# Low parts of weight tiles kept in DRAM for the later token groups, and every second high part of h cast by ScalarE

## The chip, the core and the metric

One core of one Trainium2 chip. TensorE (PE) multiplies, with its weight loads on a queue of their own (PEld); VectorE (DVE), ScalarE (ACT) and GpSimd (POOL) work element by element; SyncE (SP) issues every DMA of this kernel, in one order. The metric is the device time of one execution in microseconds. Before the change it is 1192.86 us, the median of 3 runs (1191.8 to 1195.96).

## What is computed

One layer of a backbone over 2048 latent tokens and 128 prompt tokens, width 1024:

```python
h = rmsnorm(x, norm_g) * (1 + scale[:, None]) + shift[:, None]
p = h @ w_in
qkv, g_a, beta_logit, a_logit, uv, g_b, x_c, g_c, x_d, g_d = jnp.split(p, _split_points(), axis=-1)
y_a, S_new = deltanet_branch(qkv, g_a, beta_logit, a_logit, S0, conv_qkv, a_log, dt_bias, dn_norm_g)
y_b = sgu_branch(uv, g_b, sgu_norm_g, sgu_w, sgu_b)
y_c = pool_branch(x_c, g_c, pool_w, pool_scale)
y_d = fourier_branch(x_d, g_d, fourier_w)
out = jnp.concatenate([y_a, y_b, y_c, y_d], axis=-1) @ w_out
return x + gate[:, None] * out, S_new
```

The DeltaNet branch is a gated delta rule in chunks of 64 positions, scanned forward and backward; the others are a gated chunk MLP, average pooling, and a 2-D DFT. A final rmsnorm follows.

## The kernel before

**Two parts of each operand.** h and the weights are float32. For the matmuls each is split into a high part (a cast to TensorE's fp32r type) and a low part (the value minus the high part, cast again). `mm3` (L246) forms a product from three matmuls per block of 128 inputs: high by high, high by low, low by high. So every weight tile needs a high and a low part in SBUF; both are made on the chip each time the tile is loaded.

**Token groups.** The 17 token tiles of 128 are worked in three groups: group 0 and group 1 with 6 tiles, group 2 with 4 latent tiles and the prompt. Only one group's h lies in SBUF (`hT`, high and low).

**Stages.** Phase A runs over the groups 0, 1, 2: `x_prep` and `x_fin` make h, then come the projections for the DFT and the scalars (`wxd`, 272 columns), the pooling branch (`wxc_d`, two tiles) and q, k, v (six tiles of `in_wt`), with the short convolution (L824), the chunk matrices and the triangular solve (L725, L727) on DVE. The second stage loads the other ten tiles of `in_wt` and `wv` (256 columns) for group 2, then group 1, then group 0 (`gates`, `r_b`); beside it runs the scan (`scan`), whose 34 steps read R and C from DRAM. Last come the 17 output tiles. So each tile of `in_wt` and `wxc_d`, and `wv`, is loaded three times, once for each group.

**The load of a weight tile.** `load_w` (L218) takes one of three slots (`Ring`) in `BIG`, 136 columns each, or two for a wide tile. It brings the tile in halves of 4 input blocks to a staging tile `wst`, of which there are two buffers; casts it into the slot (ACT in phase A, L242; DVE after it, L240); and subtracts to get the low part (L243: DVE for the first half, POOL for the second). The cast waits until TensorE is done with the slot's tile of three loads ago; the next DMA into a `wst` buffer waits until the subtract has read it.

**The split of h.** For each of the 8 blocks f of 128 features, `x_fin` transposes on PE, ACT writes h (L351), and `h_split` (L358) casts the high part on DVE (L361) and subtracts on DVE for even f, on POOL for odd f (L362).

**What sets the order.** The program is written stage by stage, and a scheduler places the instructions of each engine by a timeline of its own and by priorities (`tc.high_priority`). Each engine then runs its list in order, SP's DMAs too.

## Time and profile before

| | us |
|---|---|
| median of 3 runs | 1192.86 |
| the profiled execution | 1198.78 |
| its span, first to last instruction | 1197.0 |
| PE busy in the span | 1046.3 |
| DVE busy | 818.9 |
| POOL busy | 433.2 |
| ACT busy | 386.2 |

Busy time is that of one execution. Matmuls are pipelined and their ends are modelled, so a busy PE is not one at its peak, and shares of a whole span mix stages with different limits: what a change in a stage is worth is read from the rows of that stage.

### The profile page before, as it was taken

The page shows a single profiled execution, that of the slowest core. Times are in us where ns is not written, and L with a number is a line of the kernel's source. Part 1 is how long each engine was busy: PE and PEld are TensorE (multiplying, and loading weights), DVE is VectorE, ACT ScalarE, POOL GpSimd, SP SyncE. Part 2 cuts the span into 40 slices and gives each one's busy share as a digit, 9 for nine tenths or more (in the row PEclk, how much of TensorE's full clock was granted, in tenths as well). Part 3 has the DMA queues.
Part 4 walks back from the last instruction along what each step waited for, and adds up shares of the span by engine and source line. Part 5 has one row for each costly group of instructions (what it writes and reads, how often), then busy time and mean ns, then how long its engine had stood idle before and what let it go on. Part 6 is the DMA issues. An engine that isn't in the chain of part 4 may idle for free.

```text
span 1197.0 us, 27975 instructions
## 1 busy us (share of the span) xinstructions
PE 1046.3 (87%) x11351; PEld 954.6 (80%) x11351; DVE 818.9 (68%) x1837; ACT 386.2 (32%) x734; POOL 433.2 (36%) x436
## 2 busy tenths in 40 slices
PE   4689897888768789967988999888999889999997
PEld 1489786888757788955778888878899879999997
DVE  1547878699995799958865533672443398887765
ACT  1345566436675564131131111121111311111211
POOL 1338446633562245511132132232144444332212
PEclk7599897898978899988899999999999889999998
DMA  9799557854453655565268356578555655444331
GB/s 309 238 327 290 156 117 202 250 165 112 107 134 103 154 126 126 179 170 160 71 197 241 100 170 207 176 230 283 143 151 161 204 153 186 132 142 140 108 131 71
DMA packets 251395, 204.16 MB, mean 171 GB/s; under 512 B 109150, under 2 KB 218718, under 8 KB 251010
## 3 DMA queue, kind: packets, MB, share of 16 engines
q1 hardware_dynamic: 251266, 202.37, 57.7%
q8 instruction: 89, 1.46, 0.5%
q14 instruction: 40, 0.33, 0.1%
HBM read 138.86 MB, written 63.46 MB: 169 GB/s over the span
## 4 chain that ended last, share of the span: by engine, by line
PE 41%; DVE 27%; DMA 17%; issue 6%; ACT 4%; SPq 2%; POOL 2%; DVEq 0%; ACTq 0%; POOLq 0%
PE pj L250 32%; DMA wst<-in_wt_dram 4%; PE pa L1035 3%; DMA ada<-in_ada_dram 3%; DVE LL L727 3%; DVE acc L824 3%; DVE ltmp L725 3%; DMA pr<-in_cpr_dram 2%; DVE BIG L243 2%; DVE BIG L361 1%; DVE acc L871 1%; SPq L1024 1%; DVE BIG L240 1%; DVE BIG L362 1%; DVE LL L748 1%
## 5 line engine op out<-in xcount | busy, mean ns | idle before, releaser
L250 PE MATMUL pj<-BIG 128*128 128x256 f32 (+4 forms) x3888 | 630.8, 319 | 25.6 <-ACT raw L805 5.6
L250 PEld LDWEIGHTS pj<-BIG 128*128 128x128 f32 x3888 | 578.1, 201 | 50.7 <-issue 11.0
L250 PE MATMUL pj<-BIG,yh 128*128 128x256 f32 x1088 | 196.7, 286 | 1.6 <-ACT BIG L1340 0.8
L243 POOL TENSOR_TENSOR BIG<-wst,BIG 128x512 fp32r<-128x512 f32 (+1 forms) x66 | 93.3, 1414 | 215.2 <-DVE BIG L240 131.2
L250 PEld LDWEIGHTS pj<-BIG,yh 128*128 128x128 f32 x1088 | 164.7, 191 | 4.6 <-ACT BIG L1340 1.0
L250 PE MATMUL pj<-BIG,yl 128*128 128x256 f32 x544 | 140.8, 284 | 0.0
L250 PEld LDWEIGHTS pj<-BIG,yl 128*128 128x128 f32 x544 | 99.0, 191 | 0.4
L240 DVE CAST BIG<-wst 128x512 fp32r<-128x512 f32 (+2 forms) x72 | 35.0, 487 | 75.7 <-DMA wst<-in_wt_dram 35.4
L1398 POOL TENSOR_TENSOR z<-z,xs 128x1024 f32<-128x1024 f32 x16 | 40.3, 2521 | 75.8 <-DVE z L1390 66.0
L1042 POOL TENSOR_TENSOR gS<-S,sc_s 128x256 f32<-128x256 f32 x32 | 19.7, 616 | 132.1 <-DVE S L1057 109.1
L824 DVE SCALAR_TENSOR_TENSOR acc<-raw,prm,acc 128x768 f32<-128x768 f32 (+2 forms) x72 | 66.3, 942 | 1.6 <-ACT acc L822 1.6
L243 DVE TENSOR_TENSOR BIG<-wst,BIG 128x512 fp32r<-128x512 f32 (+1 forms) x66 | 49.8, 754 | 24.3 <-ACT BIG L242 20.7
L1359 ACT ACTIVATE yh<-yt 128x768 fp32r<-128x768 f32 (+1 forms) x34 | 20.5, 628 | 121.6 <-issue 65.5
L1204 ACT ACTIVATE g<-pj 128x256 f32<-128x256 f32 (+1 forms) x64 | 23.0, 397 | 109.6 <-PE pj L250 109.3
L725 DVE TENSOR_TENSOR ltmp<-LL 128x60 f32<-128x60 f32 (+14 forms) x90 | 55.5, 617 | 1.6
L727 DVE TENSOR_TENSOR LL<-LL,ltmp 128x60 f32<-128x60 f32 (+14 forms) x90 | 55.3, 615 | 1.5
L242 ACT ACTIVATE BIG<-wst 128x512 fp32r<-128x512 f32 (+1 forms) x60 | 37.7, 633 | 38.4 <-DMA wst<-in_wt_dram 17.9
L264 PE MATMUL pb<-ada,c 128*32 128x256 f32 x192 | 22.1, 566 | 31.7 <-DMA ada<-in_ada_dram 21.4
L1057 DVE TENSOR_TENSOR S<-pa,gS 128x256 f32<-128x256 f32 x34 | 14.3, 421 | 50.6 <-PE pc L1035 45.3
L1390 DVE TENSOR_TENSOR z<-pj,gbc 128x256 f32<-128x256 f32 x68 | 26.2, 420 | 29.1 <-PE pj L250 28.8
L362 POOL TENSOR_TENSOR BIG<-h,BIG 128x384 fp32r<-128x384 f32 (+2 forms) x28 | 29.1, 1041 | 44.5 <-DVE BIG L361 38.7
L1360 DVE TENSOR_TENSOR yl<-yt,yh 128x768 fp32r<-128x768 f32 (+1 forms) x34 | 40.4, 1206 | 4.1 <-ACT yh L1359 3.9
(280 smaller groups left out, 1690.2 us busy)
## 6 DMA issues: line engine op xcount, KB each, us to landing
wst<-in_wt_dram SPq DMA_DIRECT2D x96, 256.0 KB, 3.7
R<-rec_d SPq DMA_DIRECT2D x136, 128.0 KB, 3.0
ada<-in_ada_dram SPq DMA_DIRECT2D x24, 512.0 KB, 8.7
C<-com_d SPq DMA_DIRECT2D x68, 128.0 KB, 3.2
xs<-xs_d SPq DMA_DIRECT2D x16, 512.0 KB, 5.3
out_dram<-z SPq DMA_DIRECT2D x16, 512.0 KB, 3.0
x<-in_xs_dram SPq DMA_DIRECT2D x13, 512.0 KB, 6.4
xs_d<-x SPq DMA_DIRECT2D x13, 512.0 KB, 4.7
```

The costliest lines, as they stand in the source:

```text
L240: nc.vector.tensor_copy(hi[:, ks, a:a + w], st[:, :, :w])
L242: nc.scalar.activation(hi[:, ks, a:a + w], st[:, :, :w], AF.Copy)
L243: (nc.vector if k0 == 0 else nc.gpsimd).tensor_tensor(lo[:, ks, a:a + w], st[:, :, :w], hi[:, ks, a:a + w].bitcast(F32), op=ALU.subtract)
L250: nc.tensor.matmul(out, lh[a](k), rh[b](k), start=(k == first and i == 0), stop=(k == last and i == 2))
L362: (nc.gpsimd if f % 2 else nc.vector).tensor_tensor(hT[1][:, f, off:off + w], h, hi.bitcast(F32), op=ALU.subtract)
L725: nc.vector.tensor_tensor(tv, X[:, :, j, j + 1:32].unsqueeze(2).to_broadcast([128, 2, j, ni]), bc(X[:, :, 0:j, j], ni), op=ALU.mult)
L727: nc.vector.tensor_tensor(X[:, :, 0:j, j + 1:32], X[:, :, 0:j, j + 1:32], tv, op=ALU.add)
L824: nc.vector.scalar_tensor_tensor(o, raw[:, si + j:si + j + n], w[:, j:j + 1], o, op0=ALU.mult, op1=ALU.add)
L1035: nc.tensor.matmul(ps[o, q], lh(q)[hp], rh[hp, q])
L1360: nc.vector.tensor_tensor(yl[:, q], yt[:, q], yh[:, q].bitcast(F32), op=ALU.subtract)
L1390: nc.vector.tensor_tensor(z[:, ns], ps, gbc[:, cd, ns], op=ALU.mult)
L1398: nc.gpsimd.tensor_tensor(z, z, xs, op=ALU.add)
```

## The change

**Low parts.** When a tile of `in_wt`, `wxc_d` or `wv` is loaded for the first time, its low part is made as before and then stored to a DRAM tile `lo_d` of its own. When it is loaded again, `load_w` issues a DMA of the low part from DRAM straight to the slot ahead of the two `wst` DMAs, and leaves out the subtracts. `wxd` (272 columns) stays as it was. There are 19 stores and 38 such loads: 36 of a tile of 128 columns (512 KB by the sizes of its type) and two of `wv`, of 1 MB.

**h.** In `h_split`, ACT casts the high part for even f; DVE keeps the odd ones.

```diff
+            key = str(src)
+            kept = key in lo_d
+            if kept:
+                nc.sync.dma_start(out=lo.bitcast(F32), in_=lo_d[key])
...
-                    (nc.vector if k0 == 0 else nc.gpsimd).tensor_tensor(lo[:, ks, a:a + w], st[:, :, :w], hi[:, ks, a:a + w].bitcast(F32), op=ALU.subtract)
-            return hi, lo
+                    if not kept:
+                        (nc.vector if k0 == 0 else nc.gpsimd).tensor_tensor(lo[:, ks, a:a + w], st[:, :, :w], hi[:, ks, a:a + w].bitcast(F32), op=ALU.subtract)
+        if n != 272 and not kept:
+            lo_d[key] = dram.tile([128, KC, n], F32, name=f"lo_d{len(lo_d)}")
+            nc.sync.dma_start(out=lo_d[key], in_=lo.bitcast(F32))
+        return hi, lo
...
-        nc.vector.tensor_copy(hi, h)
+        if f % 2:
+            nc.vector.tensor_copy(hi, h)
+        else:
+            nc.scalar.activation(hi, h, AF.Copy)
```

**Counts by engine.** DVE's L243 goes from 66 to 26 instructions, POOL's from 66 to 26; DVE's L361 from 56 to 28, and ACT gains the other 28. SP gains 57 DMAs. ACT's table loads go from 44 to 48, since its list has another order. Changed lines of the new kernel: L236 is the load of a low part, L251 its store, L242 the `wst` DMA, L372 and L374 the casts of h on DVE and ACT, L375 the subtract of h.

**What moves: SP in phase A, the q, k, v and pooling weights of group 1.** In a row's brackets stand the semaphores it waits for; DMAHW ones are earlier DMAs. Before:

```order
L238 DMA wst<-in_wt_dram 128x4x128 [waits DMAHW2_49,DVE_49]
L302 DMA xs_d<-x 128x1024 [waits DMAHW1_49,Pool_49]
L238 DMA wst<-in_wt_dram 128x4x128 [waits Pool_49]
L302 DMA xs_d<-x 128x1024 [waits DMAHW4_49,DMAHW3_49,Pool_49]
L887 DMA raw_d<-rawc 128x768 [waits DVE_49,Activation_49]
L238 DMA wst<-in_wt_dram 128x4x128 [waits DMAHW5_49,DMAHW0_49,Pool_49]
L238 DMA wst<-in_wt_dram 128x4x128 [waits DMAHW6_49,DMAHW2_49,DVE_49]
```

After, at the same place:

```order
L236 DMA BIG<-lo_d_1093 128x8x128 [waits DMAHW6_49,PE_49]
L242 DMA wst<-in_wt_dram 128x4x128 [waits DMAHW7_49,Activation_49]
L242 DMA wst<-in_wt_dram 128x4x128 [waits DMAHW1_49,DMAHW0_49,Activation_49]
L900 DMA raw_d<-rawc 128x768 [waits DVE_49]
L577 DMA pf_d_85<-pt 48x2x64 [waits DMAHW2_49,Activation_49]
L236 DMA BIG<-lo_d_1103 128x8x128 [waits DMAHW3_49,PE_49]
L312 DMA xs_d<-x 128x1024 [waits DMAHW4_49,Pool_49]
L242 DMA wst<-in_wt_dram 128x4x128 [waits DMAHW7_49,DMAHW5_49,Activation_49]
```

The `wst` DMAs now wait for ACT's cast instead of a subtract on DVE or POOL, and the DMA of a low part, which waits for PE to leave the slot, stands between them.

**What moves: SP in the second stage, group 1, beside the scan's R and C.** Before:

```order
L1026 DMA C<-com_d 128x256 [waits DMAHW6_49,PE_49]
L1026 DMA C<-com_d 128x256 [waits DMAHW7_49]
L238 DMA wst<-in_wt_dram 128x4x128 [waits DMAHW0_49,DVE_49]
L1024 DMA R<-rec_d_78 64x512 [waits DMAHW1_49,PE_49]
L1024 DMA R<-rec_d_78 64x512 [waits DMAHW2_49]
L1024 DMA R<-rec_d_80 64x512 [waits DMAHW3_49]
L1024 DMA R<-rec_d_80 64x512 [waits DMAHW4_49]
L238 DMA wst<-in_wt_dram 128x4x128 [waits DMAHW5_49,DMAHW0_49,DVE_49]
```

After:

```order
L1039 DMA C<-com_d 128x256 [waits PE_49]
L1039 DMA C<-com_d 128x256
L236 DMA BIG<-lo_d_6462 128x8x128 [waits DMAHW4_49,PE_49]
L242 DMA wst<-in_wt_dram 128x4x128 [waits DMAHW5_49,DVE_49]
L242 DMA wst<-in_wt_dram 128x4x128 [waits DMAHW6_49,DMAHW1_49,DVE_49]
L1037 DMA R<-rec_d_78 64x512 [waits DMAHW7_49,PE_49]
L1037 DMA R<-rec_d_78 64x512 [waits DMAHW0_49]
L1037 DMA R<-rec_d_80 64x512
L1037 DMA R<-rec_d_80 64x512 [waits DMAHW2_49]
L236 DMA BIG<-lo_d_5591 128x8x128 [waits DMAHW3_49,PE_49]
```

The low part stands ahead of the R loads of a scan step, with a wait for PE of its own.

**What moves: DVE and ACT where `x_fin` makes h of group 1.** DVE before (acc is the short convolution, kt, Pp and S belong to the scalars of group 0):

```order
L361 CAST BIG<-h 128x384 x2
L362 TENSOR_TENSOR BIG<-h,BIG 128x384
L824 SCALAR_TENSOR_TENSOR acc<-raw,prm,acc 128x768
L361 CAST BIG<-h 128x384
L824 SCALAR_TENSOR_TENSOR acc<-raw,prm,acc 128x768
L601 TENSOR_REDUCE kt<-tm 128x12
L824 SCALAR_TENSOR_TENSOR acc<-raw,prm,acc 128x768
L243 TENSOR_TENSOR BIG<-wst,BIG 128x4x136
L361 CAST BIG<-h 128x384
```

ACT after, at this place:

```order
L361 ACTIVATE h<-pa,modab 128x384
L374 ACTIVATE BIG<-h 128x384
L246 ACTIVATE BIG<-wst 128x4x136
L361 ACTIVATE h<-pc,modab 128x384
L615 ACT_TABLE_LOAD
L615 ACTIVATE kt<-kt,eps 128x12
L246 ACTIVATE BIG<-wst 128x4x136
L818 ACTIVATE raw<-pj 128x392
L374 ACTIVATE BIG<-h 128x384
```

Every second cast of h stands now in ACT's list, in between its casts of weights, its evictions of PSUM (L818) and its writes of h.

## Rows read from the trace of the kernel before

**Rows 1.** The page: the chain of work that ended last, by engine and by line, as shares of the span.

```profile
PE 41%; DVE 27%; DMA 17%; issue 6%; ACT 4%; SPq 2%; POOL 2%; DVEq 0%; ACTq 0%; POOLq 0%
...
by line: PE pj L250 32.3%; issue 5.8%; DMA wst<-in_wt_dram 4.4%; PE pa L1035 3.3%; DMA ada<-in_ada_dram 2.7%; DVE LL L727 2.6%; DVE acc L824 2.6%; DVE ltmp L725 2.5%; DMA pr<-in_cpr_dram 2.1%; DVE BIG L243 1.9%; DVE BIG L361 1.1%; DVE acc L
```

**Rows 2.** Busy time of each engine in stretches of 50 us (PE, PEld, DVE, ACT, POOL with the number of instructions, then TensorE's granted clock as a share of full speed, the DMA engines' share and GB/s). The first two lie in group 0's part of phase A, the next five in the rest of it, the last two in the second stage.

```profile
150.00:200.00 50.00, 43.16 (x308) 38.50 (x308) 41.02 (x73) 34.09 (x52) 25.40 (x27) 0.86 0.71 170
200.00:250.00 50.00, 40.84 (x376) 38.70 (x376) 36.92 (x65) 21.90 (x40) 30.29 (x29) 0.93 0.73 222
250.00:300.00 50.00, 45.81 (x335) 43.11 (x334) 49.29 (x93) 25.53 (x43) 17.87 (x16) 0.93 0.47 117
300.00:350.00 50.00, 35.52 (x258) 31.22 (x256) 49.63 (x82) 33.24 (x52) 27.09 (x29) 0.84 0.55 130
350.00:400.00 50.00, 41.76 (x630) 37.77 (x631) 30.22 (x90) 26.27 (x56) 17.11 (x24) 0.84 0.42 100
400.00:450.00 50.00, 42.93 (x466) 41.01 (x466) 47.45 (x97) 30.67 (x60) 21.90 (x27) 0.87 0.64 147
450.00:500.00 50.00, 47.19 (x328) 46.10 (x328) 48.65 (x89) 16.01 (x31) 30.08 (x44) 0.97 0.52 143
650.00:700.00 50.00, 46.06 (x619) 42.15 (x621) 27.93 (x71) 6.58 (x16) 15.97 (x14) 0.97 0.40 117
850.00:900.00 50.00, 50.00 (x735) 46.89 (x735) 21.63 (x45) 6.92 (x17) 18.18 (x16) 1.00 0.50 148
```

**Rows 3.** Groups of instructions by line and shape: count, busy time in us, mean of one in ns, then the idle time ahead of them.

```profile
L243 POOL TENSOR_TENSOR BIG<-wst,BIG 128x512 fp32r<-128x512 f32 x54 | 75.9, 1406 | 167.7 <-DVE BIG L240 86.7 <-ACT BIG L242 33.0 <-PE pj L250 21.9
L243 DVE TENSOR_TENSOR BIG<-wst,BIG 128x512 fp32r<-128x512 f32 x54 | 41.4, 766 | 20.8 <-ACT BIG L242 18.0 <-PE pj L250 1.8
L242 ACT ACTIVATE BIG<-wst 128x512 fp32r<-128x512 f32 x48 | 29.9, 627 | 33.9 <-DMA wst<-in_wt_dram 17.9 <-PE pj L250 11.6 <-DMA wst<-wxc_d 4.3
L826 ACT ACT_TABLE_LOAD x12 | 15.4, 1283 | 0.7 <-DVE acc L824 0.5
L351 ACT ACTIVATE h<-pa,modab 128x384 f32<-128x384 f32 x16 | 10.5, 666 | 1.9 <-PE pa L349 1.6 <-POOL BIG L362 0.3
```

**Rows 4.** All instructions of L243 in stretches of 50 us (DVE and POOL busy, then clock, DMA share, GB/s), the two pairs of stretches of Rows 2 in which DVE is nearly full; and their sum over the whole execution.

```profile
250.00:300.00 50.00, 2.73 (x4) 6.87 (x4) 0.93 0.47 117
300.00:350.00 50.00, 2.10 (x3) 4.02 (x3) 0.84 0.55 130
400.00:450.00 50.00, 3.13 (x4) 6.25 (x4) 0.87 0.64 147
450.00:500.00 50.00, 6.21 (x6) 7.46 (x5) 0.97 0.52 143
...
sum 1200.00, DVE 49.76 POOL 93.26; mean DVE 2.07 POOL 3.89
```

**Rows 5.** The casts of L361 on DVE in the stretches from 0 to 650 us, summed.

```profile
sum 650.00, DVE 27.01; mean DVE 2.08
```

**Rows 6.** Waits of SP's queue for others, and of PE for the low parts: us in total, times, longest.

```profile
SPq L238 <- DVE BIG L243: 89.1, 26, 10.0
SPq L238 <- POOL BIG L243: 68.5, 40, 3.9
SPq L1024 <- PE pc L1035: 28.8, 15, 5.0
...
PE pj L250 <- DVE BIG L243: 5.4, 4, 2.9
```

**Rows 7.** DMA issues: count, KB each, median us from issue to landing.

```profile
wst<-in_wt_dram SPq DMA_DIRECT2D x96, 256.0 KB, 3.7
R<-rec_d SPq DMA_DIRECT2D x136, 128.0 KB, 3.0
out_dram<-z SPq DMA_DIRECT2D x16, 512.0 KB, 3.0
x<-in_xs_dram SPq DMA_DIRECT2D x13, 512.0 KB, 6.4
xs_d<-x SPq DMA_DIRECT2D x13, 512.0 KB, 4.7
```

**Rows 8.** The chain from 371 to 376 us, where group 2's weights come in: start, duration, what.

```profile
371.21 0.64 ACT BIG L242
371.87 0.70 DVE BIG L243
372.59 3.06 DMA wst<-in_wt_dram
375.68 0.64 ACT BIG L242
```

**Rows 9.** The timeline of the second stage, group 0: start, duration, instruction. 23 matmul records are those of one chunk of 24.

```profile
871.86 0.43 DVE L240 CAST BIG<-wst 128x512 fp32r<-128x512 f32 x1 [3.57 <-PE pj L250]
...
873.80 2.99 PE L250 MATMUL pj<-BIG 128*128 128x256 f32 x23
878.05 1.28 POOL L243 TENSOR_TENSOR BIG<-wst,BIG 128x512 fp32r<-128x512 f32 x1 [2.95 <-PE pj L250]
...
879.29 3.98 POOL L1250 TENSOR_TENSOR u<-u,g 128x768 f32<-128x768 f32 x2
...
880.69 0.89 DVE L240 CAST BIG<-wst 128x512 fp32r<-128x512 f32 x1 [1.08 <-DMA wst<-in_wt_dram]
```

More of the change, by code (lines that the diff above doesn't have):

```diff
@@ L242, in load_w @@
                         nc.scalar.activation(hi[:, ks, a:a + w], st[:, :, :w], AF.Copy)
-                    (nc.vector if k0 == 0 else nc.gpsimd).tensor_tensor(lo[:, ks, a:a + w], st[:, :, :w], hi[:, ks, a:a + w].bitcast(F32), op=ALU.subtract)
-            return hi, lo
+                    if not kept:
[4 more added lines that the diff above has]
+        return hi, lo
+    lo_d = {}
     def mm3(out, lh, rh, ks=range(KC), first=0, last=KC - 1):
```

## Prediction

> **What bounds the kernel now.** I read the chain of work first, then the stretches, then the groups that the change touches. The chain [rows 1] is no single engine's: PE has 41% of it, DVE 27%, DMA 17%. The stretches say where each rules [rows 2]. From 250 to 350 us and from 400 to 500 us DVE is busy 47.45 to 49.63 of 50 us, while PE has gaps and its granted clock falls to 0.84: there DVE is the bound. From 350 to 400 us nothing is full (DVE 30.22, ACT 26.27): h and the weights of group 2 are made step after step. In the second stage PE rules: 46.06 and 50.00 of 50, with DVE at 21 to 28. The output tiles load no weight through the changed code and keep their time. So the change can pay in phase A for groups 1 and 2, where DVE is full and tiles are loaded for the second and third time; in group 0 it only adds, and in the second stage it can easily cost, since PE's list has little slack there.
>
> **Part 1: subtracts that go.** 40 leave DVE and 40 leave POOL. At 766 and 1406 ns [rows 3] that is 40 x 0.766 = 30.6 us of DVE and 40 x 1.406 = 56.2 us of POOL. By place: 16 of the 38 kept loads lie in phase A (six q, k, v tiles and two pooling tiles, for two groups), with one DVE subtract each: 16 x 0.766 = 12.3 us. The other 22 loads, with 24 DVE subtracts (`wv` has two), are in the second stage: 18.4 us.
>
> What is worth what? The whole line has 49.76 us on DVE [rows 4], and 1.9% of 1197.0 = 22.7 us of it stands on the chain [rows 1], a share of 0.46. For phase A this gives 12.3 x 0.46 = 5.6 us as a low value. In the two full stretches the line has 14.17 us, its four stretches summed [rows 4], most of it of kept tiles, and where an engine is full nearly all that leaves it is gained: 12.3 us as a high value. I take 8. In the second stage PE is next in line at once. The share of 0.46 would give 18.4 x 0.46 = 8.5 us, a full PE 0; I take 3.
>
> The staging loop belongs to this term, and is not counted again. Today a turn is cast 0.64, subtract 0.70, DMA 3.06 us [rows 8], and SP waits for subtracts for 89.1 and 68.5 us before it may refill `wst` [rows 6]. A kept tile frees the buffer at the cast, 0.7 us sooner; the low part's DMA ahead of it takes about this back.
>
> POOL's 56.2 us matter in another way: the same cast took 0.43 us alone and 0.89 us while POOL worked on L1250 [rows 9]. If part of the DVE work beside those subtracts ran slower for them, it speeds up. Low end 0; high end 56.2 x 0.46 x half a DVE's pace = 12.9; I take 2, nearer to the low end, since the two casts are a single pair.
>
> **Part 2: casts of h.** Half of 27.01 us [rows 5] leaves DVE: 13.5 us. On the chain L361 has 1.1% = 13.2 us, a share of 0.49: 6.6 us saved at most. ACT gets 28 casts at about its own price for that shape, 0.63 to 0.67 us by L242 and L351 [rows 3], some 17 us, and in `x_fin` the cast now stands on the engine that also writes the next h. For two features ACT had 2 x 0.666 and DVE two casts and a subtract; after it ACT has 2 x 0.666 + 0.63 = 1.96 us, so ACT becomes as late as DVE was. Where DVE is full this gains, where `x_fin` sets the pace (350 to 400 us) it does not: between +6 of cost (ACT's queue ahead of a cast) and -6.6; I take a gain of 2.
>
> The other order of ACT's list has four more table loads, 4 x 1.283 = 5.1 us [rows 3]. ACT is busy 16 to 34 of 50 us in phase A [rows 2], so most of this is covered; cost 1, between 0 and 5.1. The Trainium skill (ScalarE: Activation LUTs, What ACT_TABLE_LOAD costs) puts a drain of some 1.38 us to each load, so that a switch is about 2.66 us. By it the four would be an estimated 10.6 us of ACT, and I would put 2 where I put 1, so the sum would be 1 us less of a gain.
>
> **Part 3: stores of low parts.** 19 DMAs on SP, eight of them in group 0, where the DMA engines are busy 0.71 to 0.73 of the time [rows 2], each behind both subtracts of its tile, which the next `wst` DMA waits for today. Nobody waits for the data until the next group, 100 us later. What they can delay is the DMAs behind them: one of this size lands in 3.0 to 6.4 us [rows 7]. If nothing of it shows, 0; if in group 0 each holds up the next by what it lands later than a `wst`, 4.7 - 3.7 = 1.0 us, 8; I take 2.
>
> **Part 4: loads of low parts.** Each waits on SP until PE has left the slot, then has to land before the third matmul of the tile. For most tiles there is time: with three slots, in phase A at least a whole tile of two chunks (48 matmuls) lies between the release of a slot and its next use, and the slots in the second stage have at least 48 matmuls, 2 x 2.99 = 6.0 us by the time of one chunk [rows 9] and scan steps besides, except one. The second `gates` tile after `wv` takes a slot that `wv` leaves, and is needed one chunk later: 3.0 us. There the present work fits: two casts and POOL's subtract, 2 x 0.43 + 1.28 = 2.1 us. A DMA of this size takes 3.0 (output), 4.7 (`xs_d`) or 6.4 us (x, at the crowded start): PE stands still for 0, 1.7 or 3.4 us, once in group 1 and once in group 0. I take the middle one: 2 x 1.7 = 3.4. For the 8 tiles with two chunks of time, 4.7 us fits and 6.4 is late by 0.4: 0 to 3. The low part of `wv`, 1 MB, I cost at nothing: it comes at the change of groups, where `r_load` brings h back by 8 DMAs and splits it on DVE, and PE needs that too; without this cover it would be a landing, some 4.7 us, twice. [...]
>
> These 22 loads are also in front of the scan's R and C on SP and on the DMA engines. R lands in 3.0 us [rows 7], and SP already waits 28.8 us in all for PE ahead of R [rows 6]. Cost 1, with the upper end under the second rival.
>
> **The sum.** Gains 8 + 3 + 2 + 2 = 15; costs 1 + 2 + 3.4 + 1 = 7.4. That is 7.6 us less than the profiled execution's 1198.78: 1191.2. The profiled execution was 5.9 us above the median of the runs, 1192.86; taken off that, 1185.3, and I say 1185.
>
> **Rivals.** *First: nothing to be seen.* PE waits for the low parts for only 5.4 us directly [rows 6], and the order of every list changes. If phase A gives the low value, 5.6, and nothing else, against the 7.4 of cost, the time is 1192.86 + 1.8 = 1194.7; with the second stage's 3 as well, 1191.7. For it: the second stage is PE's [rows 2]. Against it: two stretches of 100 us where DVE is full.
>
> *Second: slower, by the scan's supply.* Mechanism: in the second stage the low part's DMA stands ahead of R and C in SP's list, waits for PE's last use of a slot, and then moves four times as much as one R (512 against 128 KB [rows 7]). If R lands after the scan step asks for it, PE, which runs its list in order, stops with it. Each of the 22 loads would cost up to 4.7 - 3.0 = 1.7 us, 37 us if all did; with half, 19 us, less the 7.6 + 1 of the sum's other terms: about 1203. It decides from the point where the delay of R exceeds the slack of a scan step; since steps are spaced by PE's own work there, I take it for less likely. For it: SP is one queue, and PE is full.
>
> *Third: the full gain.* If DVE is as much the bound as the four stretches say, 12.3 in phase A, 6.6 from h and 8.5 in the second stage, and the low parts land in 3.0 us: 27.4 - 4 = 23.4 less, 1169.5.
>
> *That it does not do what it says* can be excluded for the counts: the lists of the new kernel have the 38 loads and 26 subtracts.
>
> **Chances.** My forecast, 1176 to 1189: 0.40. Full gain, under 1176: 0.14. Nothing to be seen, within 0.3% (about 3.6 us, what a measurement of this kernel can tell from no change): 0.19. Slower: 0.27, of which most ends below 1206. So faster 0.54, same 0.19, slower 0.27. The range for 8 in 10 runs from 1167 to 1206: it leaves out a part of the slower case and a little of the full gain.
>
> **What would show it.** Right: the DVE stretches of phase A for groups 1 and 2 shorter, the first scan step some 8 us earlier in time, SP's waits for L243 cut by more than half, PE without new waits for a DMA of `lo_d` but for one or two of 1 to 3 us behind `wv`. The cast of h: ACT in 350 to 400 us fuller, without PE waiting longer for h's low parts. Wrong: PE waiting for `lo_d` in many places of the second stage, or for R and C; the granted clock lower there; or group 0 longer by more than a few us, by its stores. The sum would also fail if the new lists put other work of DVE in front of the solve, since each engine runs in order and a term here takes the rest of the order as it was.

## The result, and the profile after

The changed kernel takes 1212.85 us, the median of 20 runs (1203.0 to 1222.85), against 1195.09 for the kernel before in as many. The ratio is 1.0143, 95% interval 1.0123 to 1.0163: slower by 17 us, where 8 us of gain were forecast. The second rival's side came true. The profiled execution was one of the two slowest of the 20, 1221.22 us at a mean granted clock of 0.910, 8.4 us above the median; so its rows are read for where the time goes, not for sums, and beside those of e2 below, which has the same low parts (1210.24 us, clock 0.918).

The page of the changed kernel: busy time, DMA traffic, and the chain by engine.

```profile
PE 1049.1 (86%) x11351; PEld 961.4 (79%) x11351; DVE 765.3 (63%) x1769; ACT 402.1 (33%) x766; POOL 372.5 (31%) x396
...
DMA packets 310675, 235.62 MB, mean 193 GB/s; under 512 B 110062, under 2 KB 277998, under 8 KB 310290
...
PE 47%; DVE 20%; DMA 17%; ACT 7%; issue 4%; SPq 3%; POOL 1%; DVEq 0%; ACTq 0%; POOLq 0%
```

DVE lost 53.6 us of work and POOL 60.7; by the counts it was 30.6 + 13.5 = 44.1 and 56.2, so what stayed on DVE ran 9.5 us quicker too. In the chain DVE fell from 27% [rows 1] to 20%, and PE rose from 41% to 47%.

The same stretches as in [rows 2], of the changed kernel.

```profile
150.00:200.00 50.00, 38.77 (x267) 33.53 (x265) 38.68 (x68) 33.56 (x56) 24.20 (x26) 0.78 0.85 212
200.00:250.00 50.00, 45.89 (x399) 44.46 (x400) 30.94 (x62) 25.11 (x46) 26.03 (x25) 0.88 0.85 252
250.00:300.00 50.00, 47.38 (x369) 45.54 (x368) 46.16 (x88) 29.09 (x46) 17.88 (x18) 0.97 0.69 172
300.00:350.00 50.00, 34.28 (x236) 31.54 (x236) 42.44 (x79) 38.64 (x65) 18.91 (x26) 0.80 0.56 128
350.00:400.00 50.00, 41.29 (x733) 37.29 (x731) 21.09 (x75) 25.82 (x59) 10.35 (x17) 0.90 0.63 153
400.00:450.00 50.00, 45.95 (x425) 43.46 (x414) 48.48 (x111) 32.68 (x65) 17.07 (x28) 0.97 0.84 200
450.00:500.00 50.00, 47.03 (x325) 46.15 (x324) 49.20 (x80) 14.02 (x23) 30.51 (x44) 0.97 0.72 209
650.00:700.00 50.00, 50.00 (x647) 45.40 (x641) 20.95 (x79) 8.79 (x24) 2.46 (x4) 1.00 0.59 173
850.00:900.00 50.00, 45.13 (x563) 41.94 (x561) 15.60 (x35) 6.58 (x15) 8.30 (x9) 0.92 0.71 193
```

Read DVE's number, the third with a count behind it, and the clock, the third number from the end. From 300 to 400 us DVE is busy 42.44 and 21.09 of 50 where it was 49.63 and 30.22. In 650 to 700 us PE is full. In 850 to 900 us, where PE was busy 50.00 at a clock of 1.00, it is now busy 45.13 at 0.92, with the DMA engines at 0.71 instead of 0.50.

Groups of the changed lines: count, busy us, mean ns, then the idle time ahead of them.

```profile
L248 POOL TENSOR_TENSOR BIG<-wst,BIG 128x512 fp32r<-128x512 f32 (+2 forms) x26 | 38.1, 1466 | 92.8 <-DVE BIG L244 48.6 <-issue 31.5 <-ACT BIG L246 6.3
L248 DVE TENSOR_TENSOR BIG<-wst,BIG 128x512 fp32r<-128x512 f32 (+2 forms) x26 | 20.9, 804 | 8.7 <-ACT BIG L246 8.4
L374 ACT ACTIVATE BIG<-h 128x384 fp32r<-128x384 f32 (+2 forms) x28 | 13.0, 464 | 0.2
L372 DVE CAST BIG<-h 128x384 fp32r<-128x384 f32 (+2 forms) x28 | 12.0, 430 | 27.7 <-ACT h L361 27.7
```

DMA issues: count, KB, median us from issue to landing (compare [rows 7]).

```profile
wst<-in_wt_dram SPq DMA_DIRECT2D x96, 256.0 KB, 4.6
BIG<-lo_d SPq DMA_DIRECT2D x36, 512.0 KB, 5.5
R<-rec_d SPq DMA_DIRECT2D x136, 128.0 KB, 3.4
lo_d<-BIG SPq DMA_DIRECT2D x18, 512.0 KB, 5.9
```

The trace tells the landing of 13 of the 38 loads of low parts: 5.5 us after the issue in the median, 4.1 to 8.9 in all. `wst` went from 3.7 to 4.6, R from 3.0 to 3.4. Waits, as in [rows 6]:

```profile
SPq L1037 <- PE pc L1048: 51.4, 15, 7.7
SPq L242 <- DVE BIG L248: 27.5, 12, 8.5
SPq L242 <- POOL BIG L248: 13.0, 10, 2.7
...
PE pc L359 <- ACT h L361: 15.4, 4, 6.0
PE pj L260 <- DMA BIG<-lo_d: 10.5, 4, 4.1
```

SP's waits for subtracts fell from 89.1 and 68.5 us to 27.5 and 13.0. Three waits are new or longer: PE stands 10.5 us before low parts and 15.4 before an h that ACT has not written, and SP waits 51.4 us instead of 28.8 for PE ahead of R. With the low parts alone (e2) PE stands 9.8 us before low parts and 11.7 before h, where before the change it is 4.3 before h, and SP waits only 31.5 us ahead of R.

Group 0's part of the second stage, the chain by line. Before, from 797 to 951 us:

```profile
by line: PE pj L250 59.0%; PE pa L1035 11.7%; DMA wos<-in_wo_dram 6.3%; DMA wst<-in_wt_dram 5.0%; DMA R<-rec_d 3.3%; issue 2.6%; DVE r L1047 2.0%; PE pc L1035 1.9%; PE pb L1258 1.9%; ACT BIG L1340 1.4%; DVE BIG L1198 1.0%; DVE BIG L1341 0.8
```

After, from 801 to 975 us, with some of its pieces (start, us, what):

```profile
by line: PE pj L260 43.6%; DMA BIG<-lo_d 11.1%; PE pa L1048 7.9%; DMA wst<-in_wt_dram 6.8%; DMA R<-rec_d 4.8%; DMA wos<-in_wo_dram 3.6%; DMA raw_d<-yd 2.7%; issue 2.6%; PE pb L1271 2.2%; DVE r L1060 1.9%; SPq L1037 1.9%; DVE BIG L244 1.3%; 
...
801.81 7.65 DMA BIG<-lo_d
864.85 6.79 DMA BIG<-lo_d
923.20 4.94 DMA BIG<-lo_d
```

The load of a low part is now on the path, with 11.1% of 174 us, some 19 us. These are the places where PE stands for one there (start, us, instruction, and in brackets how long PE stood):

```profile
809.51 2.70 PE L260 MATMUL pj<-BIG 128*128 128x256 f32 x12 [4.10 <-DMA BIG<-lo_d]
871.69 1.65 PE L260 MATMUL pj<-BIG 128*128 128x256 f32 x6 [2.31 <-DMA BIG<-lo_d]
928.18 1.09 PE L260 MATMUL pj<-BIG 128*128 128x256 f32 x7 [3.88 <-DMA BIG<-lo_d]
```

The first load, issued at 801.81, is the low part of `wv`, 1 MB. The last, issued at 923.20, came 1.1 us before PE asked for it (928.18 - 3.88 = 924.30). It had not waited for its slot: in the 6 us before, SP had waited 2.9 us for a `wst` DMA to land and 1.8 us for DVE's cast, for a `wst` DMA ahead of it in its list.

To compare kernels part by part, I count the projections' matmuls (`pj` from `BIG`, 3888 in all) in order of time: the first 1560 are phase A's, then 600, 864 and 864 of the second stage's groups 2, 1 and 0. Each number below is the time from the start of one part's first matmul to the next part's, in us, phase A's from the start of the span; the rest is the end of the scan and the output tiles, up to the start of the last matmul on a `pj` tile.

| kernel | phase A | group 2 | group 1 | group 0 | rest |
|---|---|---|---|---|---|
| before | 463.5 | 156.3 | 176.9 | 153.9 | 237.8 |
| after | 455.6 | 168.3 | 177.8 | 173.4 | 235.7 |
| e1_h_only | 465.4 | 143.0 | 183.6 | 159.0 | 241.5 |
| e2_low_only | 446.9 | 155.1 | 187.6 | 175.9 | 234.3 |
| e3_low_phase_a | 447.4 | 147.3 | 185.0 | 152.7 | 241.5 |
| e4_low_second | 462.2 | 150.4 | 170.6 | 164.3 | 243.3 |
| e5_stores_only | 456.8 | 157.9 | 174.8 | 157.0 | 238.4 |
| e6_second_firsts | 464.4 | 151.7 | 171.4 | 160.2 | 239.8 |
| e7_second_seconds | 460.3 | 158.2 | 177.1 | 161.3 | 241.3 |
| e8_h_all | 454.9 | 153.1 | 178.4 | 152.2 | 241.8 |
| e9_second_half | 460.9 | 149.6 | 173.6 | 156.0 | 241.3 |
| e10_second_pool_queue | 462.9 | 147.3 | 180.7 | 165.3 | 239.4 |
| e11_phase_a_and_h | 455.9 | 150.9 | 184.4 | 152.2 | 240.3 |
| e12_phase_a_h_all | 454.6 | 146.6 | 186.4 | 151.4 | 240.5 |
| e13_phase_a_second_half | 449.7 | 155.9 | 187.8 | 153.9 | 240.2 |
| e14_h_phase_a | 464.6 | 144.5 | 186.8 | 157.8 | 241.4 |
| e15_h_second | 463.2 | 158.9 | 176.8 | 156.8 | 237.6 |
| e16_h_odd | 460.6 | 151.7 | 185.4 | 153.5 | 241.9 |
| e17_phase_a_second_stores | 445.3 | 157.4 | 184.5 | 147.1 | 237.4 |
| e18_second_half_stores | 445.0 | 150.6 | 174.4 | 157.6 | 237.3 |

In the changed kernel phase A is 7.9 us shorter; group 2's part of the second stage is 12.0 us longer and group 0's 19.5. Two of these kernels are others once more (e14 is e1, e15 is the kernel before, see below), and by them a part repeats to within some 3 us. A part also holds whatever else the lists put between its bounds. Group 0's part before and after, with the columns of [rows 2]:

```profile
796.70:950.60 153.90, 141.66 (x1913) 132.28 (x1908) 63.50 (x136) 28.59 (x70) 56.05 (x46) 0.97 0.62 191
```

```profile
801.70:975.10 173.40, 151.54 (x2007) 140.20 (x2005) 60.80 (x131) 30.35 (x75) 42.70 (x38) 0.95 0.71 210
```

Of the 19.5 us, 9.9 are PE busy, with 94 matmuls more in this part and a clock of 0.95 instead of 0.97; the other 9.6 are PE idle, and the three waits above (10.3 us) are as much.

### The profile page after: what moved, and what is told of

It is laid out like the page before. It is cut to its first block, busy times and chain, and to the rows that moved or that the text cites. A ratio compares the mean times of both kernels' runs of the same rounds, so it can differ in the third digit from the quotient of the medians.

```text
span 1219.4 us, 27942 instructions
## 1 busy us (share of the span) xinstructions
PE 1049.1 (86%) x11351; PEld 961.4 (79%) x11351; DVE 765.3 (63%) x1769; ACT 402.1 (33%) x766; POOL 372.5 (31%) x396
## 2 busy tenths in 40 slices
DMA packets 310675, 235.62 MB, mean 193 GB/s; under 512 B 110062, under 2 KB 277998, under 8 KB 310290
## 4 chain that ended last, share of the span: by engine, by line
PE 47%; DVE 20%; DMA 17%; ACT 7%; issue 4%; SPq 3%; POOL 1%; DVEq 0%; ACTq 0%; POOLq 0%
PE pj L260 37%; PE pa L1048 3%; DMA wst<-in_wt_dram 3%; DVE ltmp L738 3%; DVE LL L740 2%; DMA pr<-in_cpr_dram 2%; DVE acc L837 2%; DMA R<-rec_d 2%; DMA ada<-in_ada_dram 2%; DMA BIG<-lo_d 2%; ACT XF L770 1%; SPq L1037 1%; PE pb L1271 1%; DMA h_d<-h 1%; DVE LL L731 1%
## 5 line engine op out<-in xcount | busy, mean ns | idle before, releaser
L260 PE MATMUL pj<-BIG 128*128 128x256 f32 (+4 forms) x3888 | 631.3, 319 | 45.3 <-DMA BIG<-lo_d 10.5
L260 PEld LDWEIGHTS pj<-BIG 128*128 128x128 f32 x3888 | 579.9, 201 | 68.5 <-issue 14.3
L244 DVE CAST BIG<-wst 128x512 fp32r<-128x512 f32 (+2 forms) x72 | 40.5, 566 | 77.6 <-DMA wst<-in_wt_dram 36.6
L837 DVE SCALAR_TENSOR_TENSOR acc<-raw,prm,acc 128x768 f32<-128x768 f32 (+2 forms) x72 | 62.7, 893 | 7.4 <-ACT acc L835 7.3
L248 POOL TENSOR_TENSOR BIG<-wst,BIG 128x512 fp32r<-128x512 f32 (+2 forms) x26 | 38.1, 1466 | 92.8 <-DVE BIG L244 48.6
L738 DVE TENSOR_TENSOR ltmp<-LL 128x60 f32<-128x60 f32 (+14 forms) x90 | 58.7, 652 | 1.6
L1066 ACT ACTIVATE xn<-pa 128x256 f32<-128x256 f32 x34 | 13.0, 383 | 123.7 <-PE pa L1048 123.3
L740 DVE TENSOR_TENSOR LL<-LL,ltmp 128x60 f32<-128x60 f32 (+14 forms) x90 | 50.9, 566 | 1.7
L1373 DVE TENSOR_TENSOR yl<-yt,yh 128x768 fp32r<-128x768 f32 (+1 forms) x34 | 43.8, 1310 | 5.0 <-ACT yh L1372 5.0
L375 POOL TENSOR_TENSOR BIG<-h,BIG 128x384 fp32r<-128x384 f32 (+2 forms) x28 | 28.3, 1012 | 53.3 <-DVE BIG L372 47.5
```

The lines of the kernel that those rows point to most:

```text
L244: nc.vector.tensor_copy(hi[:, ks, a:a + w], st[:, :, :w])
L248: (nc.vector if k0 == 0 else nc.gpsimd).tensor_tensor(lo[:, ks, a:a + w], st[:, :, :w], hi[:, ks, a:a + w].bitcast(F32), op=ALU.subtract)
L260: nc.tensor.matmul(out, lh[a](k), rh[b](k), start=(k == first and i == 0), stop=(k == last and i == 2))
L375: (nc.gpsimd if f % 2 else nc.vector).tensor_tensor(hT[1][:, f, off:off + w], h, hi.bitcast(F32), op=ALU.subtract)
L738: nc.vector.tensor_tensor(tv, X[:, :, j, j + 1:32].unsqueeze(2).to_broadcast([128, 2, j, ni]), bc(X[:, :, 0:j, j], ni), op=ALU.mult)
L740: nc.vector.tensor_tensor(X[:, :, 0:j, j + 1:32], X[:, :, 0:j, j + 1:32], tv, op=ALU.add)
```

## The experiments

Each kernel was timed beside the kernel before on the same chip; a ratio is to that kernel, with its 95% interval.

### The two halves of the change

Each is one part of the diff alone on the kernel before: the cast of h (**e1_h_only**), and the low parts (**e2_low_only**), these again only where a tile's first load is in phase A, or only after it:

```diff
-        if n != 272 and not kept:
+        if n != 272 and not kept and not Ring.late:   # e3_low_phase_a
+        if n != 272 and not kept and Ring.late:       # e4_low_second
```

> Only the cast of h: every second high part of h on ScalarE, no low part kept. Theory A (the loss is the supply of low parts in the second stage): about as before, 1193 to 1197 us, ratio 0.998 to 1.002. Theory B (ScalarE's cast delays h at the start of groups 1 and 2, as the trace of the changed kernel suggests with PE waiting 11.9 us for h between 190 and 340 us): 5 to 12 us slower, ratio 1.004 to 1.010. Theory C (the stores and their traffic): as A.

> Only the low parts kept in DRAM, all casts of h on VectorE as before. Theory A and C: most of the loss is here, ratio 1.012 to 1.020. Theory B: half of it or less, ratio under 1.008.

> Low parts kept for the tiles of phase A alone (8 stores, 16 loads), subtracts in the second stage as before, casts of h as before. Theory A: faster than before by the 8 us that phase A gained in the trace, ratio 0.990 to 0.996. Theory C (stores and traffic cost as much as the subtracts): ratio 0.999 to 1.005.

> Low parts kept for the tiles of the second stage alone (11 stores, 22 loads), phase A as before, casts of h as before. Theory A: the whole loss and more, ratio 1.014 to 1.022, with PE waiting some 10 us for the loads of low parts and the span of group 0's part of the second stage up by about 20 us. Theory B or C: under 1.008.

| kernel | median us | ratio |
|---|---|---|
| e1_h_only | 1203.80 | 1.0070 (1.0044 to 1.0096) |
| e2_low_only | 1204.13 | 1.0071 (1.0043 to 1.0100) |
| e3_low_phase_a | 1182.54 | 0.9891 (0.9853 to 0.9928) |
| e4_low_second | 1205.66 | 1.0086 (1.0054 to 1.0118) |

Both halves lose, and together make the whole loss (1.0070 x 1.0071 = 1.0141, measured 1.0143). The low parts are two changes in one: in phase A they gain 1.1%, in the second stage they lose 0.9%. Their product, 0.9976, is not what both give together, 1.0071. Waits of PE for low parts in e4:

```profile
PE pj L260 <- DMA BIG<-lo_d: 8.6, 4, 3.4
```

### Stores without loads

**e5_stores_only**: the 19 stores are issued and nothing is loaded back; all subtracts stay.

> All 19 stores of low parts, but no load of one: every subtract stays. Theory S (the stores and their traffic cost): ratio 1.003 to 1.010. Theory W or T (it is the loads in the second stage): 0.998 to 1.003, under 3 us.

1197.91 us against 1195.48, ratio 1.0036 (1.0008 to 1.0064): the stores cost 2.4 us on their own by the medians, 4.3 by the ratio, and 1 to 8 by its interval.

### Which loads of the second stage, and why

Tiles are loaded in pairs there. **e6_second_firsts** keeps the first of each pair and `wv`, **e7_second_seconds** the second, which takes the slot that was left last. **e9_second_half** keeps only blocks 4 to 7 of each low part, **e10_second_pool_queue** issues whole loads from GpSimd:

```diff
-                nc.sync.dma_start(out=lo.bitcast(F32), in_=lo_d[key])
+                nc.sync.dma_start(out=lo[:, 4:].bitcast(F32), in_=lo_d[key][:, 4:])   # e9, with `if not kept or k0 == 0:` for the subtract
+                nc.gpsimd.dma_start(out=lo.bitcast(F32), in_=lo_d[key])               # e10
```

> Second stage alone, and there only the first tile of each pair and wv kept: 6 stores, 12 loads (two of 1 MB). Their slots are free a whole pair before they are needed. Theory W (a low part lands later than PE needs it, where a slot comes free one or two chunks ahead): no loss, ratio 0.993 to 1.001, and no wait of PE for a low part. Theory T (the traffic and the place in SP's list, whatever the tile): more than half of the 1.0086 of all 22 loads, 1.004 to 1.008.

> Second stage alone, and there only the second tile of each pair kept: 5 stores, 10 loads, those whose slot comes free one or two chunks ahead of their use. Theory W: all of the loss, ratio 1.007 to 1.014, with PE waiting 8 to 12 us for low parts. Theory T: less than half of it, 1.001 to 1.005.

> Second stage only, and of each low part only blocks 4 to 7 are kept and loaded (256 KB instead of 512 KB); blocks 0 to 3 are subtracted on DVE as in the kernel before. If the loss of the second stage (ratio 1.0086 with whole low parts) comes from PE standing before a low part that has not landed, most of it goes: the bytes are halved and their first use comes 12 matmuls (some 1.5 us by 2.99 us for a chunk of 24) later, so PE waits under 2 us for `lo_d` in all, and the ratio is 0.999 to 1.004. If it comes from the DMA's place in SP's list ahead of R, C and `wst`, the place stays and the ratio stays at 1.005 to 1.009, with few waits for `lo_d`.

> Low parts kept in the second stage only, as in the run that gave 1.0086, but their 22 loads are issued by GpSimd and not by SyncE: SP's list has no wait for a slot ahead of R, C and `wst`. By the queue theory the loss goes: ratio under 1.003, SP's wait for PE ahead of R back near 28.8 us or below. By the landing theory it stays: the load can still not start before PE has left the slot, so PE waits 8 us or more for `lo_d` and the ratio is 1.006 or more. GpSimd may add its own: its list waits for PE, and the scan's work behind it is late.

| kernel | median us | ratio |
|---|---|---|
| e6_second_firsts | 1200.58 | 1.0045 (1.0018 to 1.0072) |
| e7_second_seconds | 1207.38 | 1.0090 (1.0058 to 1.0122) |
| e9_second_half | 1192.50 | 0.9992 (0.9961 to 1.0023) |
| e10_second_pool_queue | 1206.25 | 1.0093 (1.0058 to 1.0129) |

Waits of PE for low parts, first of e6, then of e7:

```profile
PE pj L261 <- DMA BIG<-lo_d: 1.7, 1, 1.7
```

```profile
PE pj L261 <- DMA BIG<-lo_d: 14.5, 3, 7.2
```

Landing of the loads in e4 and in e9, us from issue, smallest, median and largest (the traces tell it for 8 of 22 loads in e4 and for 2 of 22 in e9):

```profile
DMA to landing us min/median/max: 3.9/5.5/6.9
```

```profile
DMA to landing us min/median/max: 3.5/3.6/3.6
```

And in e10 the waits, and the landing of a load:

```profile
POOL BIG L236 <- PE pj L260: 69.9, 12, 11.8
PE pj L260 <- DMA BIG<-lo_d: 7.4, 7, 1.5
...
BIG<-lo_d POOLq DMA_DIRECT2D x20, 512.0 KB, 7.0
```

The seconds of the pairs lose most, with PE standing 14.5 us in three places; 10 loads of them cost as much as all 22. Halves are asked for half a chunk later, and the two that can be read landed in 3.6 us: no wait of PE for `lo_d` is left in e9, and the loss is gone, though e9 halves the bytes of the loads too. GpSimd's queue frees SP's list of the loads and doesn't help, but it is no clean test of SP's list: GpSimd itself waits 69.9 us for PE, a load then takes 7.0 us, and PE still stands 7.4 us. So most of the loss of the second stage goes with PE standing before a low part that has not landed. That a load could not start earlier is not shown. In e7, where PE stands longest, SP comes to the load only behind four R of a scan step, does not wait for PE there, and PE asks for the low part 0.1 us after the issue. PE, then SP:

```profile
834.26 1.65 PE L261 MATMUL pj<-BIG 128*128 128x256 f32 x6 [7.16 <-DMA BIG<-lo_d]
```

```profile
823.64 3.28 SPq L1035 DMA_DIRECT2D R<-rec_d  x4
827.02 0.55 SPq L236 DMA_DIRECT2D BIG<-lo_d  x1
```

So the place in SP's list is a part of the cause: not R late behind the loads, but a load late behind R. And waits of PE are not the whole loss: e6 loses 0.45% with only 1.7 us of them, which its expectation had given to the traffic and the place in SP's list.

### Casts of h

On the kernel before: all high parts on ACT (**e8_h_all**), every second one in phase A only (**e14_h_phase_a**) or in the second stage only (**e15_h_second**), and the odd features on ACT (**e16_h_odd**). The edits of e14 and e15 do not part anything: all 56 casts of `h_split` lie in phase A (L361, 48.5 to 374.5 us of the kernel before), and in the second stage `r_load` splits h by lines of its own. So e14 is the program of e1, and e15 that of the kernel before, with the same lists. On the kernel with low parts kept in phase A: the cast of the change (**e11_phase_a_and_h**), and all casts (**e12_phase_a_h_all**).

```diff
+        if f % 2:                       # e1, e11: even f on ACT
+        if f % 2 or Ring.late:          # e14
+        if f % 2 or not Ring.late:      # e15
+        if f % 2 == 0:                  # e16
             nc.vector.tensor_copy(hi, h)
+        else:
+            nc.scalar.activation(hi, h, AF.Copy)   # e8, e12: always
```

> No low part kept; ScalarE casts all the high parts of h, not every second one (double dose). If ScalarE's queue is what the cast of h costs: twice the loss, ratio 1.012 to 1.020. If the loss of the half dose came from the new order of the lists and not from ScalarE's work: anything between 0.995 and 1.010, with no relation to the dose.

> The kernel before with ScalarE casting the high part of every second feature of h in phase A only; in the second stage all are on DVE. If the loss of the h cast (1.007) lies in phase A, where ScalarE's list holds the cast behind other work that waits for PE and DVE's subtract waits for the cast: 1.004 to 1.010. If it lies in the second stage, 0.997 to 1.002.

> The kernel before with ScalarE casting every second feature of h in the second stage only. By the phase A theory 0.997 to 1.003; if the loss is in the second stage, 1.004 to 1.010.

> The kernel before with ScalarE casting the high part of the odd features of h, DVE that of the even ones: as many casts on ScalarE as in the run that gave 1.007, but the subtract behind a cast of ScalarE is now GpSimd's, and the one of DVE follows DVE's own cast. If the loss is DVE's list standing at a subtract until ScalarE has cast, it goes: 0.996 to 1.003. If it is ScalarE's added work, or any list in which the two engines alternate, 1.004 to 1.010.

> The changed kernel without low parts in the second stage: low parts kept in phase A (0.9891 alone) and every second high part of h cast by ScalarE (1.007 alone). If the two add, 0.9891 x 1.007 = 0.996. If the loss of the h cast was an accident of the lists that the scheduler happened to make from it, it need not come back: 0.985 to 0.992. If ScalarE is now the engine that phase A waits for, since the low parts took DVE out of the way, it is worse than the sum: 0.999 or more.

> Low parts kept in phase A (0.9891 alone) and all high parts of h cast by ScalarE (1.0004 alone). If they add, 0.9895. If ScalarE becomes what phase A waits for, more than 0.995 with PE waiting longer for h (L361). If DVE's relief pays only once `x_fin` is short too, below 0.986.

| kernel | median us | ratio |
|---|---|---|
| e8_h_all | 1197.34 | 1.0004 (0.9975 to 1.0032) |
| e14_h_phase_a | 1205.96 | 1.0098 (1.0078 to 1.0118) |
| e15_h_second | 1197.32 | 1.0019 (0.9996 to 1.0041) |
| e16_h_odd | 1200.96 | 1.0066 (1.0047 to 1.0084) |
| e11_phase_a_and_h | 1192.89 | 0.9967 (0.9940 to 0.9993) |
| e12_phase_a_h_all | 1191.93 | 0.9961 (0.9937 to 0.9985) |

The two expectations on where the loss lies rest on a mistake of mine, and e14 and e15 can only say how well a ratio repeats: 1.0070 and 1.0098 for the program of e1, and 1.0019 for the kernel before beside itself. The loss itself stands, but little of it in phase A: this ends at 465.4 and 464.6 us, against 460.3 to 464.4 in the seven kernels with the lists of before there (before, e4, e6, e7, e9, e10, e15). What else differs comes in the second stage, which holds no cast of `h_split`: group 2's part is 12 to 13 us shorter than before, and what follows it is 15 to 17 us longer. ACT's table loads are not it: e1 has 44, as before, and e8 has 50 and loses nothing. My theory that DVE stands at a subtract until ACT has cast falls with e16, where that wait is GpSimd's and the loss stays. What goes with the loss is PE waiting in `x_fin` for ACT to write h. Waits of PE in e1, then in e8:

```profile
PE pa L349 <- ACT h L351: 6.5, 5, 3.3
PE pc L349 <- ACT h L351: 4.6, 3, 3.2
```

```profile
PE pc L349 <- ACT h L351: 4.0, 4, 2.0
```

Before, this wait is 4.3 us in all. It is 11.1 in e1, 10.8 in e14, 7.1 in e16 and 4.0 in e8, where nothing is lost. It is no proof, since e3 has 11.3 us of it and gains; what costs time in e1, and why all casts on ACT are cheaper than half of them, stays open. On top of the low parts of phase A, as in the changed kernel, the cast costs in phase A itself: this ends at 455.9 (e11) and 454.6 us (e12) instead of 447.4 (e3), and PE's wait for h is 16.9 and 18.6 us instead of 11.3. The ratio of e11 is what the two single runs give (0.996); that of e12, 0.9961, is worse than what they give (0.9895). There DVE waits in a row; its timeline in e11, where group 1's h is made:

```profile
208.19 1.15 DVE L375 TENSOR_TENSOR BIG<-h,BIG 128x392 fp32r<-128x392 f32 x1 [3.71 <-ACT BIG L374]
212.51 0.57 DVE L375 TENSOR_TENSOR BIG<-h,BIG 128x392 fp32r<-128x392 f32 x1 [2.08 <-ACT BIG L374]
223.76 0.17 DVE L925 COPY lg<-pj 128x16 f32<-128x16 f32 x1 [8.59 <-ACT xdt L924]
```

The first two rows are DVE standing at a subtract of h until ACT has cast; in the third it stands 8.59 us for ACT's `xdt`, which stands behind a weight cast in ACT's list. ACT had stood 5.86 us for PE before that cast, and 1.89 us more for PE before `xdt`.

### Both stages together

**e13_phase_a_second_half** keeps whole low parts in phase A and halves in the second stage. **e17_phase_a_second_stores** keeps them in phase A and only stores them in the second stage. **e18_second_half_stores** is e13 with the second stage's stores halved too:

```diff
+            nc.sync.dma_start(out=lo_d[key][:, 4 * Ring.late:], in_=lo[:, 4 * Ring.late:].bitcast(F32))   # e18, the store
```

> Whole low parts kept in phase A (0.9891 alone), and in the second stage only blocks 4 to 7 of each low part (0.9992 alone); h as in the kernel before. If the two add, 0.988. Whole low parts in both stages gave 1.0071 where the sum was 0.9976, so there was something that only both together showed. If that was PE standing before low parts that had not landed, in lists that the two together made tighter, half low parts are free of it: 0.985 to 0.992. If it is the gain of phase A that gets lost whenever the second stage's SP list is longer, 0.995 to 1.003.

> Low parts kept in phase A (0.9891 alone); in the second stage the 11 low parts of group 2 are stored as in the change, but never loaded, and all their subtracts stay. If the phase A gain is lost to these stores (in the run with halves, group 2's part of the second stage ended 11 us later than with phase A alone, and weight DMAs had 14% of its chain instead of 5%): 0.997 to 1.003, with group 2's part again some 10 us late. If it is lost to the loads in groups 1 and 0: 0.987 to 0.992.

> As the run with whole low parts in phase A and halves in the second stage (1.0018), but the second stage's stores are halves too (256 KB; there they were whole). If the bytes of the stores cost the phase A gain: 0.993 to 0.998. If the loads do, or the mere place of the stores in the lists: 1.000 to 1.004.

| kernel | median us | ratio |
|---|---|---|
| e13_phase_a_second_half | 1196.59 | 1.0018 (0.9997 to 1.0038) |
| e17_phase_a_second_stores | 1188.26 | 0.9950 (0.9928 to 0.9972) |
| e18_second_half_stores | 1174.49 | 0.9835 (0.9809 to 0.9860) |

Phase A keeps its gain in all three (449.7, 445.3, 445.0 us against 463.5); it is paid back later. Stores alone take half of it (0.9950 instead of 0.9891), between what I expected of stores and of loads. Halving the stores gives back 1.8%, more than I expected, and makes the fastest kernel of the study. The chain from 447 to 625 us, group 2's part and the first 20 to 30 us of group 1's, by line, in e13, then in e18:

```profile
by line: PE pj L260 17.6%; DMA wst<-in_wt_dram 13.9%; DVE ltmp L735 11.1%; DVE LL L737 11.1%; DMA hr<-h_d 7.1%; issue 5.2%; DVE LL L758 4.2%; DVE XT L758 3.2%; DVE BIG L244 3.0%; DVE BIG L248 2.9%; DMA ada<-in_ada_dram 2.5%; DVE Pf L693 1.7
```

```profile
by line: PE pj L260 20.6%; DVE ltmp L735 11.9%; DVE LL L737 10.3%; issue 7.9%; DMA wst<-in_wt_dram 4.8%; DVE BIG L244 3.5%; DMA C<-com_d 3.0%; ACT XF L767 2.9%; DMA ada<-in_ada_dram 2.3%; DVE LL L728 2.2%; DVE acc L881 2.1%; DVE XT L758 2.0
```

And the stretch from 450 to 620 us, with the columns of [rows 2], in e13, then in e18:

```profile
450.00:620.00 170.00, 132.42 (x1677) 117.51 (x1676) 131.79 (x224) 39.66 (x73) 50.78 (x61) 0.85 0.66 189
```

```profile
450.00:620.00 170.00, 140.87 (x1775) 125.63 (x1776) 132.72 (x233) 42.84 (x89) 44.23 (x56) 0.89 0.64 186
```

With whole stores, DMAs of weights and of h (`hr`) have 21% of that chain; with halves, weights have 4.8% and PE is busy 8 us more in the same stretch. But by the table only 5.3 of the 18 us between the two after phase A lie in group 2; 13.4 lie in group 1, where nothing is stored (9.7 of them PE busy, with 2137 matmuls instead of 2009 in this part). So the bytes of the stores are a part of it at most. The two also differ in PE's waits for low parts, in e13, then in e18:

```profile
PE pj L260 <- DMA BIG<-lo_d: 7.4, 4, 4.8
```

```profile
PE pj L260 <- DMA BIG<-lo_d: 1.9, 3, 0.7
```

So halves are not free of such waits everywhere, which I had expected them to be: the 4.8 us of e13 are a wait for the half of `wv` at the start of group 0.

Every edit also makes the scheduler write other lists: the scan's first step starts at 640.0 us before and at 616.4 in the changed kernel. That this counts is seen in group 2's part, where low parts are only stored. With the low parts of phase A kept, it takes 155.1 to 157.4 us with whole stores (e2, e13, e17), 150.6 with halves (e18) and 147.3 without (e3). With phase A as before it is the other way round: 147.3 to 150.4 us with whole stores (e4, e9, e10), 156.3 and 158.9 without (before, e15). Which part of the 1.8% is bytes, which is the waits and which is the list stays open.

## Why the prediction was wrong

**Part 4, loads of low parts, is the step that failed first.** It put 3.4 us on PE's stops before low parts: one late tile in each of two groups, the others in time, and the low part of `wv` at nothing. PE stands 10.5 us before low parts in the changed kernel, 9.8 in e2 and 8.6 in e4. Low parts kept in the second stage cost 9 us alone (e4: 1205.66 against 1196.78), where a gain of 3 in Part 1 had stood against 4.4 of cost here. Three sizes were wrong. `r_load` did not cover `wv`: PE stood 4.1 us for its low part at the start of group 0, and 3.4 in e4. I took 4.7 us for a landing, as the middle of three rows [rows 7]; it is 5.5, and up to 8.9. And the window of 6.0 us counts from PE leaving the slot, while SP may come to the load later: 1.1 us before PE asked at 923.20, 0.1 us in e7. e7 and e9 show the mechanism that I had described and undersized, PE before a low part that has not landed; e6 shows that it is not the whole cost.

For a DMA that GpSimd issues, the Trainium skill (DMA: Bandwidth & Descriptors, Anatomy of one DMA — SWDGE (gpsimd) path) has a fit of 2.0 us and 1 us for each 436 KB, an estimated 3.2 us for 512 KB. GpSimd's loads in e10 took 7.0 us beside this kernel's other DMAs, so the trace does not agree, and the measurement decides.

**The second rival had the right sign and the mechanism the wrong way round.** It priced R and C late behind the loads in SP's list. But SP's wait for PE ahead of R is 31.5 us in e2 and 36.5 in e4, which lose, and 31.5 in e9, which does not; it is 51.4 in the changed kernel alone. What SP's list held up was a load of a low part, behind R (e7) or `wst` (923.20). With halves, shorter and asked for later, at the same place in it (e9) the loss goes.

**Part 1 was too small in phase A and wrong in the second stage.** I took 8 of 12.3 us. The five kernels that keep low parts there and leave h alone (e2, e3, e13, e17, e18) have one and the same list in phase A and end it at 445.0 to 449.7 us, against 460.3 to 464.4 with the list before: some 16 us. e3 is 1.1%, 13 us, faster in all. That is about my full value or above it. A part of it may be the list, since other lists that load no low part end phase A at 454.9 (e8) to 465.4 us (e1). The staging loop, which I had folded in as even, is the likely reason for more: SP's waits for subtracts in phase A are 59.4 us before and 10.4 in e3. No run has tried it alone. In the second stage the 3 us of gain are not to be seen beside the loads.

**Part 2, casts of h, had the wrong sign.** A gain of 2 was forecast, a loss of 7 is measured (e1: 1203.80 against 1196.78), and on top of phase A's low parts 8 us of phase A (e11). The +6 end of the bound was the right one. In e11 the waits agree with its mechanism, ACT's queue: PE waits for h, and DVE for casts and tiles behind them. In e1 the cause is open. The price of the cast itself was near: 28 took 13.0 us where I had put some 17. ACT's work alone is not the cost on the kernel before, where all casts on ACT cost nothing (e8). The 1 us for table loads is not seen apart in any run.

**Part 3, stores, was about right alone and not in the sum.** 2 us were forecast, 2 to 4 measured (e5). I said that nobody waits for the data. On top of phase A's gain the stores took some 0.6% (e17 against e3, two intervals that touch at 0.9928); that weights wait behind them is likely by e13's chain, and not shown.

**The sum itself failed.** Of the profiled 22 us of loss up to the last matmul, phase A gives 7.9 back, group 0 takes 19.5, half of it PE idle before low parts, and group 2 takes 12.0. This last is in the changed kernel's profile alone: e2, with the same stores, has 155.1 us there against 156.3 before. The sum took the lists as given. Where low parts of both stages meet, the products of the single runs miss the joint ones by 1 to 1.4% (e2: 0.9976 against 1.0071; e13: 0.988 against 1.0018); the low parts and the cast of the change multiply as they should (1.0141 against 1.0143). So some 11 us of the loss come from the two stages together, and their cause is open. The last paragraph of the prediction names new lists as a way to fail, but gave it no price in the range: 1206 was too low an upper end.

## What to carry to other kernels

Trade an engine's work for a DMA only where the buffer is free for longer than the DMA needs to land in that stage: here whole tiles paid in phase A (e3, 0.9891) and not in the second stage, where halves did beside them in one kernel (e18, 0.9835) and not in another (e13, 1.0018). Price a new load by the crowded landings of its size, and ask of each load when its buffer is free and when the issuing queue comes to it, not only when its data is wanted. See from the lists that an edit changes what it is meant to: two runs here were other kernels once more. Where a scheduler rewrites all lists at each edit, split a change by stage and time each piece and the joint: one that gains alone may be lost in company.

## What had not been expected of the hardware

A DMA's landing hung on more than its size. The output's 512 KB land in 3.0 us [rows 7], the low part's in 5.5 (e4, eight landings), and half a low part in 3.6 (e9, two). By the pages of the two kernels the change adds 310675 - 251395 = 59280 packets and 31.46 MB, 531 bytes each: low parts go in small pieces. Whether that is the reason was not tried. The same 512 KB issued by GpSimd took 7.0 us (e10). In the changed kernel a cast of h took 464 ns on ACT and 430 on DVE, each over 28 of the same shapes: there was little to choose between them.
